# One token tile's gates by scatter DMAs in place of one-hot matmuls, in a hybrid attention and PEER encoder layer

## The chip, the cores and the metric

The kernel runs on one core of a Trainium2 chip. The metric is the device time of one execution in microseconds (us), here the median of three runs of the kernel before. One more execution was recorded by the hardware profiler, and every row shown below is from it. TensorE (PE) does matmuls, VectorE (DVE), ScalarE (ACT) and GpSimd (POOL) elementwise work; SyncE (SP), ACT and POOL issue DMAs.

## The reference

Two sequences, 256 prompt tokens and 512 sample tokens of width 1024, go through one encoder layer: RMS norm, one large projection, banded and dilated attention, gates and an output projection, and then a PEER layer. The change lies in the PEER layer of the sample. There each token picks, for each of 8 heads, 16 experts out of 16384, and adds gate times gelu(u·h) times v of each:

```python
idx = (e1 * PEER_KEYS + e2).reshape(T, PEER_HEADS * PEER_TOPK)
g = jax.nn.softmax(top, axis=-1).reshape(T, PEER_HEADS * PEER_TOPK)
...
u = expert_u[ic]
a = jax.nn.gelu(jnp.einsum('ted,td->te', u, tc, ...), approximate=False)
vv = expert_v[ic]
return jnp.einsum('te,ted->td', (gc * a).astype(tc.dtype), vv)
```

So a token has 128 pairs of expert and gate; two heads can pick the same expert, and then their gates add up. The result is to be that of fp32, which the kernel gets from three fp32r matmuls of high and low parts.

## The kernel before, in words

**Stages.** The prompt's front (norm, projection, attention, output projection, query and top 16) runs from 0 to about 315 us of the span, the sample's front to about 886 us, woven with the prompt's PEER layer. That layer gathers: `gather` (L790 to L816) fetches with one indirect DMA per slot the u row, later the v row, of 128 tokens (128 rows, 512 KB, issued by POOL at L799), and DVE multiplies it in at L806 or L814. 512 such gathers last nearly to the end of the kernel; they are the filler that is woven into all that follows.

**The sample's PEER layer** is dense. Each expert is computed for all 512 tokens. (1) The u blocks (`stage1`, L730): 128 blocks of 128 experts; each loads 512 KB of u (`ur`, by SP), is split into `uh` (ACT) and `ul` (DVE, L140), takes 24 matmuls of 128x512 into `pu`, a gelu (L740), and is stored to `ad` in DRAM. `uh` and `ul` have four buffers each. Eight blocks run first; the rest, from the generator `ua`, are woven into (2) and (3).

(2) The picks (`pick`, L634): for each of four tiles of 128 sample tokens, DVE finds the 128 experts and gates. POOL computes a table of candidate indices `ce` (L653, L655) that DVE needs further on in the same pick. At its end the pick turns indices and gates into five tables `sl` with a transpose (L695 to L701).

(3) The gate matrix (`gbuild`, L704): one row of 16384 experts per token, nonzero at the token's picks. It is built as one fp32 matmul per token, of two one-hot 128x128 matrices (`o1` with the expert's upper index, `o2` with its lower index times the gate, built at L712 to L722 on DVE and ACT), which leaves two PE records per token, 1024 in all. ACT copies the result (`p_g`) into `gs` and stores it by 2 MB DMAs into `gd`, four for each token tile.

(4) The dense stage (`dense`, L743): for each of 128 blocks of experts SP loads v (`vr`), the gelu values (`gl` from `ad`), and for each eight blocks the gates (`gt` from `gd`, 2 MB); DVE multiplies `gl` with `gt` at L761, the product and v are split into two parts each, and 24 matmuls go into the accumulators `held`.

**What sets the order.** `ORDER` (L40) lists the picks ("p") and gate tiles ("b"). `fill` (L818) advances a stage and takes one u block for so much of its work (`UP`, `UB`); `weave` takes `GB` gathers per unit of gate work, and `GV` gathers per unit of the dense stage. A scheduler then orders each engine's instructions; each engine runs its own list in order, so an instruction that waits holds back all that follow it on that engine. A gather also waits for an `anchor` (the last gelu or split issued when it was written) that paces it.

Of the kernel before, what the change touches and what calls it, by code (L numbers as in the profile page):

```python
# [21 lines left out]
D = 1024  # L22
# [17 lines left out]
IPW = 0.4  # L40
MU = 0.9
PGP, PGS = (0.5, 0.45)
ORDER, SLB = ('pppbpbbb', 3)
U0, UP, UB = (8, 0.45, 1.0)
GB, GV = (2.4, 2.0)


@with_exitstack
def tile_peer(ctx: ExitStack, tc: tile.TileContext, a: dict):
# [21 lines left out]
    ident = cp.tile([128, 128], F32, name="ident")  # L71
    make_identity(nc, ident)
    iota = cp.tile([128, 128], F32, name="iota")
    posx = cp.tile([128, NCAND], BF16, name="posx")
    ropeC = cp.tile([128, 6, 16], F32, name="ropeC")
    ropeS = cp.tile([128, 6, 16], F32, name="ropeS")
# [4 lines left out]
    def consts():  # L81

        nc.sync.dma_start(ropeC, a["ropeC"])
        nc.sync.dma_start(ropeS, a["ropeS"])
        g16 = cp.tile([128, 4, 16], F32, name="g16")
        nc.sync.dma_start(g16, a["gains"][:, 0:16].unsqueeze(0).broadcast_to([128, 4, 16]))
        gc = cp.tile([128, 4], F32, name="gc")
        for h in range(2):
            nc.sync.dma_start(gc[64 * h:64 * h + 64, :], a["gains"].rearrange("k d -> d k"))
            ve.memset(gc[64 * h:64 * h + 16, :], 1.0)  # L90
        for i, k in enumerate(("k_norm_a", "q_norm_a", "q_norm_b", "k_norm_b")):
            c = cp.tile([128, 6, 16], F32, name="rc" + k)
            s = cp.tile([128, 6, 16], F32, name="rs" + k)
            g = g16[:, i:i + 1, :]
            ve.tensor_tensor(c, ropeC, g.broadcast_to([128, 6, 16]), op=ALU.mult)
            ve.tensor_tensor(s[:, :, 0:8], ropeS[:, :, 0:8], g[:, :, 8:16].broadcast_to([128, 6, 8]), op=ALU.mult)
            ve.tensor_tensor(s[:, :, 8:16], ropeS[:, :, 8:16], g[:, :, 0:8].broadcast_to([128, 6, 8]), op=ALU.mult)
            rope[k] = (c, s)
            gcol[k] = gc[:, i:i + 1]
        nc.sync.dma_start(sink, a["sink"].unsqueeze(0).broadcast_to([128, 8]))  # L100
        ve.tensor_scalar_mul(nsink, sink, -1.0)
        nc.sync.dma_start(iota, a["iota"])
        nc.sync.dma_start(posx, a["posx"])
        yield 0

    def gain(pool, k):
# [11 lines left out]

    xs = dr.tile([S_S, D], F32, name="xs")
    sgd = dr.tile([2, 2, 4, 128, 512], F32, name="sgd")  # L120
    gd = dr.tile([S_S // GCH, 128, 128, GCH], F32, name="gd")

    anchor, turn, tog = [None], [0], [0]

# [205 lines left out]
    def front(seq):  # L330
# [6 lines left out]
        with ExitStack() as fs:  # L337
# [23 lines left out]
            with tc.tile_pool(name="att" + seq, bufs=1, reuse_waits="tile") as ap_:  # L361
# [170 lines left out]
                                         es.unsqueeze(2).broadcast_to([128, 4, 64]), op=ALU.mult)  # L532

                if seq == "p":
                    more = chain(norm1("s", tTh, tTl, "right"), gates_pre(PIECES, Th, Tl, nt, put),
                                 gates_pre(PIECES[:GS[0]], tTh, tTl, 4, put_s))
                else:
                    more = gates_pre(PIECES[GS[1]:], Th, Tl, nt, put_s)
# [95 lines left out]
    def pick(pool, seq, t, vv, iu):  # L634
# [47 lines left out]
        wt = pool.tile([128, 8, 16], F32, tag="wt", name="wt", bufs=1)  # L682
        ve.tensor_tensor(wt, tv, tv[:, :, 0:1].broadcast_to([128, 8, 16]), op=ALU.subtract)
        gates(pool, wt)
        ei = pool.tile([128, 128], I32, tag="ei", name="ei", bufs=1)
        ve.tensor_copy(ei, ex.rearrange("p h s -> p (h s)"))
        ii = pool.tile([128, 128], I32, tag="ii", name="ii", bufs=1)
# [12 lines left out]
        for j in range(1, 3):  # L700
            ac.mul(sl[t][2 + j], p[:, j * 128:(j + 1) * 128], -1.0)  # L701
        yield 2

    def gbuild(pool, t):  # L704
        for c in range(128 // GCH):
            gs = pool.tile([128, 128, GCH], F32, tag="gs", name="gs", bufs=2)
            for q in range(0, GCH, 4):
                p = (ps_tr, ps_o)[q // 4 % 2]("p_g")
                t4 = c * GCH + q
                if q % 8 == 0:  # L710
                    o1 = pool.tile([128, 8, 128], F32, tag="o1", name="o1", bufs=B1)
                    ve.tensor_tensor(o1, iota.unsqueeze(1).broadcast_to([128, 8, 128]),  # L712
                                     sl[t][0][:, t4:t4 + 8].unsqueeze(2).broadcast_to([128, 8, 128]), op=ALU.is_equal)
                for j in range(4):
                    tk = t4 + j
                    tg = {"a": "o2a", "v": "o2"}[BY[tk % len(BY)]]
                    o2 = pool.tile([128, 128], F32, tag=tg, name=tg, bufs=B2 if tg == "o2" else B3)
                    if tg == "o2a":
                        ac.activation(o2, iota, AF.Abs, bias=sl[t][3][:, tk:tk + 1])
                        ac.activation(o2, o2, AF.Relu, bias=sl[t][2][:, tk:tk + 1], scale=sl[t][4][:, tk:tk + 1])  # L720
                    else:
                        ve.tensor_scalar(o2, iota, sl[t][1][:, tk:tk + 1], sl[t][2][:, tk:tk + 1], op0=ALU.is_equal, op1=ALU.mult)  # L722
                    pe.matmul(p[:, j * 128:(j + 1) * 128], lhsT=o1[:, q % 8 + j, :], rhs=o2, start=True, stop=True)
                ac.copy(gs[:, :, q:q + 4].rearrange("p e t -> p t e"), p.rearrange("p (t e) -> p t e", e=128))
                yield 0.6
            nc.scalar.dma_start(gd[t * (128 // GCH) + c], gs)

    ad = dr.tile([128, 128, S_S], F32, name="ad")

# [13 lines left out]
    def dense(pv_, psd):  # L743
# [4 lines left out]
        def stage2(j):  # L748
            g, b = divmod(j, GRP)
            if b == 0:  # L750
                gts[g] = pv_.tile([128, S_S // GCH, GRP, GCH], F32, tag="gt", name="gt", bufs=2)
                nc.sync.dma_start(gts[g], gd[:, :, g * GRP:(g + 1) * GRP, :].rearrange("c p e t -> p c e t"))
            vr = pv_.tile([128, D], F32, tag="vr", name="vr", bufs=5)
            nc.sync.dma_start(vr, vrows[j])
            ga = pv_.tile([128, S_S], F32, tag="gl", name="gl", bufs=4)
            nc.sync.dma_start(ga, ad[j])
            vh = pv_.tile([128, D], F32R, tag="vh", name="vh", bufs=3)
            vl = pv_.tile([128, D], F32R, tag="vl", name="vl", bufs=3)
            split(vh, vl, vr)
            gv = ga.rearrange("p (c t) -> p c t", t=GCH)  # L760
            ve.tensor_tensor(gv, gv, gts[g][:, :, b, :], op=ALU.mult)  # L761
            ph = pv_.tile([128, S_S], F32R, tag="ph", name="ph", bufs=3)
            pl = pv_.tile([128, S_S], F32R, tag="pl", name="pl", bufs=3)
            anchor[0] = split(ph, pl, ga)
            return ph, pl, vh, vl
# [101 lines left out]
    with tc.tile_pool(name="gb", bufs=1, reuse_waits="tile") as gpool:  # L867
        slp.append(gpool)
        gp2.append((gpool, 2))
        P = [pick(pks["s"][1], "s", t, *tops["s"][t]) for t in range(4)]  # L870
        B = [gbuild(gpool, t) for t in range(4)]
        due = [0.0]
        it = {"p": iter(P), "b": iter(B)}
        for k in ORDER:
            g = next(it[k])
            fill(weave(g, gg, GB) if k == "b" else g, ua, UP if k == "p" else UB, due)
        run(ua)
        gp2.append((None, 0))
    pks["s"][0].__exit__(None, None, None)
# [29 lines left out]
def _layout(inputs):  # L909
# [26 lines left out]
    o["ropeS"] = np.concatenate([-s, s], axis=1).astype(np.float32).reshape(6, 128, 16).transpose(1, 0, 2)  # L936
    import ml_dtypes
    o["posx"] = np.broadcast_to(np.arange(NCAND).astype(ml_dtypes.bfloat16), (128, NCAND))
    o["iota"] = np.broadcast_to(np.arange(128, dtype=np.float32), (128, 128))
    o["maskA_s"], o["maskB_s"], o["maskO_s"] = _masks(_SEQ_S, _PERM_S[:128], 4)  # L940
    o["maskA_p"], o["maskB_p"], o["maskO_p"] = _masks(_PERM_P, _PERM_P[:128], 2)
# [22 lines left out]
```

## Time and profile before

| | us |
|---|---|
| median of 3 runs | 2473.23 (2470.12 to 2475.72) |
| the profiled execution | 2468.71 |
| its span, first to last instruction | 2466.9 |
| PE busy in the span | 2350.8 (95%) |
| DVE busy | 1886.5 (76%) |
| ACT busy | 1076.1 (44%) |
| POOL busy | 812.1 (33%) |

Read it as follows: the profiled execution lies 4.5 us under the median of the runs, and 1.8 us of it lie outside the span. Shares of busy time are means over stages with different limits, so the rows below are taken stage by stage: from about 960 to 1054 us the picks and u blocks run, from 1054 to about 1600 the gates, u blocks and gathers, to 1725 the last u blocks and the turn to the dense stage, and from there the dense stage with gathers. Where PE's busy time equals the length of its window, PE has no idle time in it, and where the window is longer, the rest is PE waiting.

### The profile page before, as it was taken

To read this page: it belongs to the slowest core of one execution; us is meant where nothing else is said; L and a number is where in the kernel's file an instruction comes from. 1 tells how busy PE (TensorE), PEld (TensorE's weight loads), DVE (VectorE), ACT (ScalarE), POOL (GpSimd) and SP (SyncE) were. 2 spreads that over 40 slices of the span, in tenths; PEclk is the share of its full clock that TensorE was granted. 3 is DMA by queue.
4 is the path that set the end of the run, shared out by engine and by line. 5 is a ranking of instruction groups with operands and counts; after the bars stand their busy time and mean duration, and the time that the engine had idled before them with its cause. 6 is when DMAs were issued, how large, how long until landed. Compare 5 with 4: busy or idle time off the path is not lost. (4 is left out here: it accounts for less than half of the span.)

```text
span 2466.9 us, 34172 instructions
## 1 busy us (share of the span) xinstructions
PE 2350.8 (95%) x11926; PEld 1964.5 (80%) x11926; DVE 1886.5 (76%) x4013; ACT 1076.1 (44%) x1848; POOL 812.1 (33%) x624
## 2 busy tenths in 40 slices
PE   8998998999998999999999999997999999999999
PEld 6787877877887888888888888876888777777777
DVE  6765699677688889978579889853787888789873
ACT  5764435434433344367466666732222222222222
POOL 0000320345555401044144544420444443444310
PEclk9999999989998999999999999999999999999999
DMA  6423542467787434479789999995899999999972
GB/s 214 145 87 128 179 136 73 151 224 224 271 280 262 137 107 137 152 289 370 250 305 372 358 352 341 339 375 211 322 392 368 343 349 352 356 353 371 376 268 103
DMA packets 246365, 642.79 MB, mean 261 GB/s; under 512 B 22576, under 2 KB 77488, under 8 KB 244144
## 3 DMA queue, kind: packets, MB, share of 16 engines
q1 hardware_dynamic: 151728, 305.02, 36.4%
q0 software_dynamic: 73728, 268.47, 30.0%
q10 hardware_dynamic: 20736, 67.12, 6.8%
q8 instruction: 94, 1.54, 0.3%
q14 instruction: 79, 0.65, 0.1%
HBM read 561.60 MB, written 77.59 MB: 259 GB/s over the span
## 5 line engine op out<-in xcount | busy, mean ns | idle before, releaser
L799 POOL DMA_INDIRECT gr<-u,pidx x256 | 329.0, 1285 | 558.9 <-ACT ph L139 168.1
L799 POOL DMA_INDIRECT gr<-v,pidx x256 | 333.4, 1302 | 459.9 <-ACT ph L139 196.2
L144 PE MATMUL held<-vh,ph 128*128 128x512 f32 x1024 | 403.0, 394 | 31.3 <-ACT ph L139 30.7
L144 PE MATMUL pu<-tTh,uh 128*128 128x512 f32 x1024 | 407.4, 398 | 14.2 <-ACT uh L139 14.2
L146 PE MATMUL pu<-tTh,ul 128*128 128x512 f32 x1024 | 401.3, 392 | 4.1 <-DVE ul L140 4.1
L806 DVE SCALAR_TENSOR_TENSOR gr<-gr,tok 128x1024 f32<-128x1024 f32 x256 | 330.8, 1301 | 96.7 <-DMA gr<-u,pidx 96.5
L145 PE MATMUL held<-vl,ph 128*128 128x512 f32 x1024 | 400.8, 391 | 0.0
L145 PE MATMUL pu<-tTl,uh 128*128 128x512 f32 x1024 | 400.6, 391 | 0.0
L814 DVE SCALAR_TENSOR_TENSOR x<-gr,act,x 128x1024 f32<-128x1024 f32 x256 | 327.4, 1279 | 42.5 <-DMA gr<-v,pidx 40.6
L146 PE MATMUL held<-vh,pl 128*128 128x512 f32 x1024 | 314.9, 389 | 0.0
L144 PEld LDWEIGHTS held<-vh,ph 128*128 128x128 f32 x1024 | 193.9, 189 | 78.3 <-ACT ph L139 37.2
L140 POOL TENSOR_TENSOR wlo<-wraw,whi 128x1024 fp32r<-128x1024 f32 x51 | 128.6, 2522 | 376.8 <-ACT whi L139 373.8
L139 ACT CAST vh<-vr 128x1024 fp32r<-128x1024 f32 x128 | 134.5, 1051 | 257.0 <-PE held L146 154.2
L144 PEld LDWEIGHTS pu<-tTh,uh 128*128 128x128 f32 x1024 | 193.8, 189 | 53.2 <-ACT uh L139 15.9
L140 DVE TENSOR_TENSOR vl<-vr,vh 128x1024 fp32r<-128x1024 f32 x128 | 156.5, 1222 | 102.4 <-ACT vh L139 98.4
L146 PEld LDWEIGHTS pu<-tTh,ul 128*128 128x128 f32 x1024 | 193.3, 189 | 46.2 <-DVE ul L140 6.1
L145 PEld LDWEIGHTS held<-vl,ph 128*128 128x128 f32 x1024 | 193.8, 189 | 40.0
L146 PEld LDWEIGHTS held<-vh,pl 128*128 128x128 f32 x1024 | 192.2, 188 | 40.0
L145 PEld LDWEIGHTS pu<-tTl,uh 128*128 128x128 f32 x1024 | 193.5, 189 | 37.6
L139 ACT CAST whi<-wraw 128x1024 fp32r<-128x1024 f32 x137 | 143.8, 1050 | 167.7 <-DMA wraw<-w_in 52.7
L139 ACT CAST uh<-ur 128x1024 fp32r<-128x1024 f32 x128 | 133.8, 1050 | 175.7 <-PE pu L145 92.7
L139 ACT CAST ph<-gl 128x512 fp32r<-128x512 f32 x128 | 79.4, 620 | 267.0 <-DVE gl L761 106.5
(400 smaller groups left out, 4565.5 us busy)
## 6 DMA issues: line engine op xcount, KB each, us to landing
ur<-ublk SPq DMA_DIRECT2D x128, 512.0 KB
vr<-v SPq DMA_DIRECT2D x128, 512.0 KB
wraw<-w_in SPq DMA_DIRECT2D x80, 512.0 KB
gd<-gs ACTq DMA_DIRECT2D x16, 2048.0 KB
gt<-gd SPq DMA_DIRECT2D x16, 2048.0 KB
gl<-ad SPq DMA_DIRECT2D x128, 256.0 KB
wraw<-w_query SPq DMA_DIRECT2D x32, 512.0 KB
wraw<-w_out SPq DMA_DIRECT2D x16, 512.0 KB
```

The lines of the kernel that those rows point to most:

```text
L139: i = ac.copy(hi, src)
L140: eng.tensor_tensor(lo, src, hi.bitcast(F32), op=ALU.subtract)
L144: pe.matmul(out, lhsT=lh, rhs=rh, start=first, stop=False)
L145: pe.matmul(out, lhsT=lh, rhs=rl, start=False, stop=False)
L146: pe.matmul(out, lhsT=ll, rhs=rh, start=False, stop=last)
L799: st = gp.indirect_dma_start(out=g, out_offset=None, in_=tab, in_offset=bass.IndirectOffsetOnAxis(ap=pidx[t][:, s:s + 1], axis=0))
L806: ve.scalar_tensor_tensor(g, g, 1.0, tok, op0=ALU.mult, op1=ALU.mult, accum_out=act[:, s:s + 1])
L814: ve.scalar_tensor_tensor(xt, g, act[:, s:s + 1], xt, op0=ALU.mult, op1=ALU.add)
```

## The change

Token tile 0 no longer goes through the gate matmuls. Its pick makes an index `si` = expert * 128 + token (the constant `pcol` is the token's number) and a copy of the gates `w0`, and no tables `sl`. A generator `scatter` then issues on POOL 128 indirect DMAs, one per slot, each of which adds 128 gates of 4 bytes into 128 cells of `gx` in DRAM. All 128 write `gx`, so the program makes each wait until the one before it has landed. Before that `gx` is zeroed: `clear` sets a 128x1024 tile to zero and stores it 16 times (512 KB each, issued by POOL), as filler of the prompt's attention, ahead of the sample's norm. `gbuild` runs for tiles 1 to 3 only, and `gd` shrinks to 12 stores. The dense stage loads `gt` in two DMAs (512 KB from `gx`, 1.5 MB from `gd`) and multiplies in two steps of 128 and 384 columns. `ORDER` has one "b" less, and `UB`, `GB` and the new `SC` set how many u blocks, gathers and scatters go to a unit of gate work.

```diff
@@ -40,9 +40,9 @@
 IPW = 0.4
 MU = 0.9
 PGP, PGS = (0.5, 0.45)
-ORDER, SLB = ('pppbpbbb', 3)
-U0, UP, UB = (8, 0.45, 1.0)
-GB, GV = (2.4, 2.0)
+ORDER, SLB = ('pppbpbb', 3)
+U0, UP, UB = (8, 0.45, 1.33)
+GB, GV, SC = (3.1, 2.0, 2.25)
 
 
 @with_exitstack
...
@@ -118,7 +120,9 @@
 
     xs = dr.tile([S_S, D], F32, name="xs")
     sgd = dr.tile([2, 2, 4, 128, 512], F32, name="sgd")
-    gd = dr.tile([S_S // GCH, 128, 128, GCH], F32, name="gd")
+
+    gx = dr.tile([128 * 128 * 128, 1], F32, name="gx")
+    gd = dr.tile([(S_S - 128) // GCH, 128, 128, GCH], F32, name="gd")
 
     anchor, turn, tog = [None], [0], [0]
 
@@ -532,7 +536,7 @@
                                          es.unsqueeze(2).broadcast_to([128, 4, 64]), op=ALU.mult)
 
                 if seq == "p":
-                    more = chain(norm1("s", tTh, tTl, "right"), gates_pre(PIECES, Th, Tl, nt, put),
+                    more = chain(clear(), norm1("s", tTh, tTl, "right"), gates_pre(PIECES, Th, Tl, nt, put),
                                  gates_pre(PIECES[:GS[0]], tTh, tTl, 4, put_s))
                 else:
                     more = gates_pre(PIECES[GS[1]:], Th, Tl, nt, put_s)
@@ -682,6 +686,14 @@
         wt = pool.tile([128, 8, 16], F32, tag="wt", name="wt", bufs=1)
         ve.tensor_tensor(wt, tv, tv[:, :, 0:1].broadcast_to([128, 8, 16]), op=ALU.subtract)
         gates(pool, wt)
+        if t == 0:
+            si = pool.tile([128, 128], I32, tag="si", name="si", bufs=1)
+            ve.tensor_scalar(si, ex.rearrange("p h s -> p (h s)"), 128.0, pcol, op0=ALU.mult, op1=ALU.add)
+            w0 = pool.tile([128, 128], F32, tag="w0", name="w0", bufs=1)
+            ac.copy(w0, wt.rearrange("p h s -> p (h s)"))
+            slots.extend((si, w0))
+            yield 2
+            return
         ei = pool.tile([128, 128], I32, tag="ei", name="ei", bufs=1)
         ve.tensor_copy(ei, ex.rearrange("p h s -> p (h s)"))
         ii = pool.tile([128, 128], I32, tag="ii", name="ii", bufs=1)
@@ -700,6 +712,26 @@
         for j in range(1, 3):
             ac.mul(sl[t][2 + j], p[:, j * 128:(j + 1) * 128], -1.0)
         yield 2
+
+    slots = []
+
+    def scatter():
+
+        si, wt = slots
+        for k in range(128):
+            gp.indirect_dma_start(out=gx, out_offset=bass.IndirectOffsetOnAxis(ap=si[:, k:k + 1], axis=0),
+                                  in_=wt[:, k:k + 1], in_offset=None, compute_op=ALU.add)
+            yield 1
+
+    def clear():
+
+        z = gpl.tile([128, D], F32, tag="gr", name="zero", bufs=3)
+        gp.memset(z, 0.0)
+        v = gx.rearrange("(p q d) o -> q p (d o)", p=128, d=D)
+        for q in range(16):
+            st = gp.dma_start(v[q], z)
+            tc.add_manual_dep(st.ins, anchor[0].ins.name, SYNC, reason="pace")
+            yield 0.1
 
     def gbuild(pool, t):
         for c in range(128 // GCH):
@@ -723,7 +755,7 @@
                     pe.matmul(p[:, j * 128:(j + 1) * 128], lhsT=o1[:, q % 8 + j, :], rhs=o2, start=True, stop=True)
                 ac.copy(gs[:, :, q:q + 4].rearrange("p e t -> p t e"), p.rearrange("p (t e) -> p t e", e=128))
                 yield 0.6
-            nc.scalar.dma_start(gd[t * (128 // GCH) + c], gs)
+            nc.scalar.dma_start(gd[(t - 1) * (128 // GCH) + c], gs)
 
     ad = dr.tile([128, 128, S_S], F32, name="ad")
 
@@ -748,8 +780,12 @@
         def stage2(j):
             g, b = divmod(j, GRP)
             if b == 0:
-                gts[g] = pv_.tile([128, S_S // GCH, GRP, GCH], F32, tag="gt", name="gt", bufs=2)
-                nc.sync.dma_start(gts[g], gd[:, :, g * GRP:(g + 1) * GRP, :].rearrange("c p e t -> p c e t"))
+                gt = pv_.tile([128, S_S * GRP], F32, tag="gt", name="gt", bufs=2)
+                g0 = gt[:, 0:128 * GRP].rearrange("p (e t) -> p e t", t=128)
+                g1 = gt[:, 128 * GRP:].rearrange("p (c e t) -> p c e t", e=GRP, t=GCH)
+                nc.sync.dma_start(g0, gx.rearrange("(p e t) o -> p e (t o)", e=128, t=128)[:, g * GRP:(g + 1) * GRP, :])
+                nc.sync.dma_start(g1, gd[:, :, g * GRP:(g + 1) * GRP, :].rearrange("c p e t -> p c e t"))
+                gts[g] = g0, g1
             vr = pv_.tile([128, D], F32, tag="vr", name="vr", bufs=5)
             nc.sync.dma_start(vr, vrows[j])
             ga = pv_.tile([128, S_S], F32, tag="gl", name="gl", bufs=4)
@@ -757,8 +793,9 @@
             vh = pv_.tile([128, D], F32R, tag="vh", name="vh", bufs=3)
             vl = pv_.tile([128, D], F32R, tag="vl", name="vl", bufs=3)
             split(vh, vl, vr)
-            gv = ga.rearrange("p (c t) -> p c t", t=GCH)
-            ve.tensor_tensor(gv, gv, gts[g][:, :, b, :], op=ALU.mult)
+            gv = ga[:, 128:].rearrange("p (c t) -> p c t", t=GCH)
+            ve.tensor_tensor(ga[:, 0:128], ga[:, 0:128], gts[g][0][:, b, :], op=ALU.mult)
+            ve.tensor_tensor(gv, gv, gts[g][1][:, :, b, :], op=ALU.mult)
             ph = pv_.tile([128, S_S], F32R, tag="ph", name="ph", bufs=3)
             pl = pv_.tile([128, S_S], F32R, tag="pl", name="pl", bufs=3)
             anchor[0] = split(ph, pl, ga)
@@ -868,12 +905,14 @@
         slp.append(gpool)
         gp2.append((gpool, 2))
         P = [pick(pks["s"][1], "s", t, *tops["s"][t]) for t in range(4)]
-        B = [gbuild(gpool, t) for t in range(4)]
+        B = [gbuild(gpool, t) for t in range(1, 4)]
+        sc = (x for f in (scatter,) for x in f())
         due = [0.0]
         it = {"p": iter(P), "b": iter(B)}
         for k in ORDER:
             g = next(it[k])
-            fill(weave(g, gg, GB) if k == "b" else g, ua, UP if k == "p" else UB, due)
+            fill(weave(weave(g, gg, GB), sc, SC) if k == "b" else g, ua, UP if k == "p" else UB, due)
+        run(sc)
         run(ua)
         gp2.append((None, 0))
     pks["s"][0].__exit__(None, None, None)
```

POOL's list at the end of the picks: `ce` is the candidate table of a pick, `gr` a gather's tile; `pidx_85` and `pidx_86` are the prompt tiles' indices. Before:

```order
L653 TENSOR_TENSOR ce<-fi,i_11830 128x8x3
L653 TENSOR_TENSOR ce<-fi,i_11830 128x8x2 x3
L655 TENSOR_TENSOR ce<-i_11830,fi 128x8x8
L799 DMA gr<-u,pidx_85 128x1024 x22
L799 DMA gr<-v,pidx_85 128x1024 x128
L799 DMA gr<-u,pidx_86 128x1024 x128
```

After the change; `gx<-w_9658,si` is a scatter of `w0` by the index `si`:

```order
L657 TENSOR_TENSOR ce<-fi,i_12120 128x8x3
L657 TENSOR_TENSOR ce<-fi,i_12120 128x8x2 x3
L659 TENSOR_TENSOR ce<-i_12120,fi 128x8x8
L722 DMA gx<-w_9658,si 2097152x1 x20
L836 DMA gr<-u,pidx_86 128x1024
L722 DMA gx<-w_9658,si 2097152x1 x2
L836 DMA gr<-u,pidx_86 128x1024 x2
L722 DMA gx<-w_9658,si 2097152x1
L836 DMA gr<-u,pidx_86 128x1024 x2
L722 DMA gx<-w_9658,si 2097152x1
```

Where the gathers followed the last `ce` directly, 20 scatters now stand between, and two groups of 12 stand ahead of the two last `ce` tables, so 44 scatters are ahead of the first gather of this stage. Behind it one or two scatters stand between every one to four gathers.

SP's list at the turn from u blocks to the dense stage, from its second load of `gt` on (`ur` u blocks, `vr` v blocks, `gl` gelu values). Before, 14 `ur` loads stand directly ahead of the first `gt`, and these follow later:

```order
L754 DMA vr<-v 128x1024
L752 DMA gt<-gd 128x16x256
L732 DMA ur<-ublk 128x1024 x2
L754 DMA vr<-v 128x1024
L756 DMA gl<-ad 128x512
```

After the change, from the store of the first prompt tile's output on:

```order
L853 DMA y<-x_81 128x1024
L764 DMA ur<-ublk 128x1024 x19
L786 DMA gt<-gx 128x1024
L787 DMA gt<-gd 128x12x256
L790 DMA vr<-v 128x1024
L792 DMA gl<-ad 128x512
```

The last eight `ur` loads (two here, six some rows further on) stood behind loads for the dense stage; now all 128 stand ahead of the first `gt`, which waits for the last scatter.

## Rows read from the trace of the kernel before

**Rows 1.** The page: the span, its busy engines, and GB/s in the 40 slices.

```profile
span 2466.9 us, 34172 instructions
...
PE 2350.8 (95%) x11926; PEld 1964.5 (80%) x11926; DVE 1886.5 (76%) x4013; ACT 1076.1 (44%) x1848; POOL 812.1 (33%) x624
...
GB/s 214 145 87 128 179 136 73 151 224 224 271 280 262 137 107 137 152 289 370 250 305 372 358 352 341 339 375 211 322 392 368 343 349 352 356 353 371 376 268 103
```

**Rows 2.** Windows: stretch, length, busy PE, PEld, DVE, ACT, POOL, then clock, DMA share, GB/s.

```profile
120.00:315.00 195.00, 179.19 (x1234) 160.01 (x1232) 120.70 (x380) 100.53 (x186) 25.33 (x11) 0.98 0.40 131
960.00:1054.00 94.00, 94.00 (x425) 77.94 (x424) 92.73 (x228) 39.43 (x69) 6.78 (x18) 1.00 0.45 149
1054.00:1600.00 546.00, 546.00 (x2904) 469.95 (x2903) 441.46 (x652) 363.77 (x662) 238.82 (x170) 1.00 0.90 331
1600.00:1725.00 125.00, 108.12 (x469) 87.50 (x467) 58.25 (x79) 37.76 (x49) 21.53 (x18) 0.93 0.81 300
1725.00:1950.00 225.00, 224.31 (x990) 185.68 (x990) 175.03 (x257) 64.81 (x81) 101.17 (x77) 1.00 0.96 355
1950.00:2370.00 420.00, 393.03 (x1711) 320.68 (x1710) 345.24 (x380) 117.31 (x145) 175.95 (x142) 1.00 0.97 357
```

**Rows 3.** Windows of the u blocks without gates, and with gates.

```profile
900.00:1050.00 150.00, 150.00 (x666) 124.16 (x665) 149.22 (x459) 61.57 (x96) 11.76 (x36) 1.00 0.47 151
1250.00:1600.00 350.00, 350.00 (x1892) 302.29 (x1891) 302.96 (x440) 243.81 (x447) 162.16 (x119) 1.00 0.94 348
```

**Rows 4.** Windows, the same stretch, instructions on tile `p_g` alone (one-hot matmuls).

```profile
1250.00:1600.00 350.00, 85.46 (x692) 84.95 (x691) 97.12 (x87) 1.00 0.94 348
```

**Rows 5.** Lines by form: mean ns of one for two DVE operations.

```profile
L722 DVE TENSOR_SCALAR o<-iota,sl,sl 128x128 f32<-128x128 f32 x320 | 97.0, 350 | 17.7 <-PE p_g L723 15.2 <-PE pu L146 1.5
...
L761 DVE TENSOR_TENSOR gl<-gl,gt 128x512 f32<-128x512 f32 x128 | 87.4, 685 | 23.3 <-DMA gl<-ad 23.0
```

**Rows 6.** Timeline of POOL: start, length, idle before and its releaser.

```profile
982.59 3.07 POOL L653 TENSOR_TENSOR ce<-fi,i 128x128 f32<-128x128 f32 x8 [29.96 <-DVE pr L674]
...
1054.06 1.64 POOL L799 DMA_INDIRECT gr<-u,pidx  x1 [33.69 <-ACT ga__10423 L740]
1062.18 2.66 POOL L799 DMA_INDIRECT gr<-u,pidx  x1 [6.48 <-ACT ga__10507 L740]
...
1068.35 0.94 POOL L799 DMA_INDIRECT gr<-u,pidx  x1 [0.30 <-issue]
```

**Rows 7.** Timeline of DVE at the turn from picks to gates.

```profile
954.40 0.21 DVE L686 CAST ei<-ex 128x128 int32<-128x128 f32 x1
...
1053.66 1.22 DVE L140 TENSOR_TENSOR ul<-ur,uh 128x1024 fp32r<-128x1024 f32 x1
...
1059.75 1.23 DVE L806 SCALAR_TENSOR_TENSOR gr<-gr,tok 128x1024 f32<-128x1024 f32 x1 [2.33 <-DMA gr<-u,pidx]
...
1069.15 1.23 DVE L806 SCALAR_TENSOR_TENSOR gr<-gr,tok 128x1024 f32<-128x1024 f32 x1 [5.13 <-DMA gr<-u,pidx]
```

**Rows 8.** Timelines of POOL and DVE, two gathers while the DMAs are little loaded.

```profile
444.50 1.05 POOL L799 DMA_INDIRECT gr<-u,pidx  x1 [5.48 <-ACT whi L139]
450.99 0.94 POOL L799 DMA_INDIRECT gr<-u,pidx  x1 [5.44 <-DVE ssq L382]
...
448.98 1.23 DVE L806 SCALAR_TENSOR_TENSOR gr<-gr,tok 128x1024 f32<-128x1024 f32 x1 [3.10 <-DMA gr<-u,pidx]
...
455.81 1.23 DVE L806 SCALAR_TENSOR_TENSOR gr<-gr,tok 128x1024 f32<-128x1024 f32 x1 [1.45 <-DMA gr<-u,pidx]
```

**Rows 9.** Waits of DVE, 1054 to 1600 us: total, times, longest.

```profile
DVE x L814 <- DMA gr<-v,pidx: 40.6, 23, 6.0
...
DVE gr L806 <- DMA gr<-u,pidx: 19.6, 6, 5.1
```

**Rows 10.** Waits of PE, 1590 to 1760 us, in the same columns.

```profile
PE pu L144 <- ACT uh L139: 13.5, 3, 9.7
```

## What the change is predicted to do

> **What bounds the kernel now.** I began with the page: PE is busy for 2350.8 of 2466.9 us, so the kernel is mostly bound by matmuls, and a cut in PE work can pay [rows 1]. But shares are means, so I read the windows by stage. From 1054 to 1600 us, where the gates are built, PE is busy in all 546.00 us, and from 960 to 1054 in all 94.00: whatever leaves PE there shortens the kernel, and whatever makes it wait there lengthens it [rows 2]. The DMAs are loaded to 0.90 with gates and to 0.45 before them; POOL works 238.82 of 546 us. At 1600 to 1725, the turn to the dense stage, PE is idle for 16.9 us at a clock of 0.93. In the dense stage PE is busy in 393.03 of 420 us. Next I asked the timeline where POOL and DVE pass from picks to gates, since the change puts its new work there [rows 6, 7]. DVE is full in that stretch (149.22 of 150 us, PE 150.00) [rows 3]. At 1053.66 it makes one more `ul`, and at 1059.75 it uses the first gather, issued at 1054.06.
>
> **What the change removes: the one-hot matmuls.** Without gates, PE passes 666 matmuls in 150 us, 0.2252 us each. With gates it passes 1892 in 350 us, of which 692 are on `p_g` [rows 3, 4]. The other 1200 take 270.2 us, so one of `p_g` takes (350 - 270.2)/692 = 0.115 us. Tile 0 has 128 tokens of two records, 256: 29.5 us less, in a stretch where PE never waits. The 32 one-hot DVE and ACT sets that go with them lie beside PE, and so do the four 2 MB stores.
>
> **What it adds: a serial chain on POOL.** Each of 128 scatters waits until the one before has landed, and POOL works its list in order, so behind a waiting scatter stand the `ce` tables of tiles 2 and 3, which DVE needs for its picks, and all gathers, which DVE uses ahead of further `ul`, and PE waits for `ul`. 44 scatters stand ahead of the first gather of this stage. The period P of one is not in the trace. The nearest row is a gather at light load: issued at 444.50 and used at 448.98, and 450.99 and 455.81, so 4.48 and 4.82 us, 4.65 in the mean, from issue to the moment DVE stops waiting for it [rows 8]. A gather moves 524288 bytes; at the page's best slice, 392 GB/s [rows 1], that is 1.34 us, which a scatter of 512 bytes does not have. POOL takes 0.30 us from one issue to the next [rows 6]. So P = 4.65 - 1.34 + 0.30 = 3.6 us. The bounds: below, issue alone, 0.94 + 0.30 = 1.24 us, if landing cost nothing [rows 6]; above, a gather in the loaded stretch, 1062.18 to 1069.15, 6.97 us [rows 6, 7], which stands also for 128 small read and add steps costing as much as 128 rows. I take 3.6 because this stretch is loaded to 0.45 only, near the light case.
>
> The Trainium skill, "DMA: Bandwidth & Descriptors", section "Anatomy of one DMA — SWDGE (gpsimd) path", gives a fixed cost of about 2.0 us per DMA, most of it the receipt from the memory written, plus bytes over 436 GB/s. By it a gather would take 3.2 us, where the rows have 4.65. As an estimate from that page, with 0.94 us of issue ahead, P would be 2.94 and the sum near 2460 instead of 2489. No row here is of a scatter, and on the gather the row disagrees with the rule by 1.4 us, so I go by the rows.
>
> Now the stall. The index is ready at the place of the `ei` of before, 954.40 [rows 7], so the chain starts at 955. 44 periods and about 7 us for the two `ce` groups behind it (3.07 us and a little each [rows 6]) put the first gather at 955 + 44 × 3.6 + 7 = 1120; 5.7 us later (1054.06 to 1059.75) DVE has it: 1126 instead of 1059.75, 66 us late. `uh` and `ul` have four buffers, so PE can work through four blocks, 4 × 24 × 0.2252 = 21.6 us, before it waits. The stall is 66 - 21.6 = **45 us**; each 1 us of P moves it by 44, and below P = 2.58 there is none. At P = 6.97 it is 193. The u blocks have no other source of work for PE here, since gates and `ul` stand behind the same DVE instruction.
>
> **The other parts.** The turn at 1600: SP's list now has all `ur` loads ahead of the first `gt`, where eight stood behind loads for the dense stage. Of the idle 16.9 us PE waited 13.5 for `uh`, behind those loads [rows 2, 10]. I take half of 16.9 back, -8.5; bounds 0 and -16.9. The last scatter, which the first `gt` awaits, is at the list's end ahead of 229 gathers and should be done by then.
>
> The other 84 scatters lie among the gathers: 84 × (0.94 + 0.30) = 104 us more on POOL, which has 307 free in 546 [rows 2]. DVE waits 40.6 + 19.6 = 60 us for gathers there now, and PE for none of it [rows 9]; half as many DMAs again (84 beside 170) may add 30. I charge a quarter, +7, since the lead is used up by the stall; bounds 0 and 30.
>
> Dense stage: 9 gathers more than before are left for it (229 for 220). PE's idle 27 us over 142 gathers is 0.19 each: +2. The product in two steps costs DVE 0.350 for 128 columns [rows 5] and, by the slope (685 - 350)/384 = 0.87 ns, 0.573 for 384: 0.24 more, 128 times, 31 us on an engine with 75 of 420 free [rows 2, 5]. PE hides it: 0; if not, the 6% in which PE waits make it 2.
>
> Clearing writes 8.4 MB in the prompt's front, where the DMAs are loaded to 0.40 [rows 2]: 0. If each of 16 stores held up its stretch for issue and transfer, 16 × (0.94 + 1.34) = +36. DVE's `si` replaces five operations of a pick: 0.
>
> **Sum.** -29.5 + 45 - 8.5 + 7 + 2 = +16. On the profiled execution, 2468.7, that is 2484.7; on the median of the runs, which lies 4.5 higher and which I forecast, 2473.2 + 16 = **2489**.
>
> **The rivals.**
> - *B, the chain is cheap.* If P is 2.6 or less, the first gather is there before PE has used up its lead, and the whole gain of the matmuls stays: -29.5 - 8.5 + 7 + 2 = -29, **2444**. For it: 512 bytes are next to nothing beside 512 KB. Against it: no indirect DMA in the rows is that quick. The price at P = 3.6 is 45 us, the point from which it decides 2.58. With P up to 3.1 the kernel is still faster by over 0.2%. The rule of the Trainium skill cited above, in "Anatomy of one DMA — SWDGE (gpsimd) path", would end in this case.
> - *C, a scatter costs what a loaded gather does.* 128 cells in 128 places, each read, added to and written back, may take as long as rows of 4 KB: P = 6.97, 193 in place of 45, **2637**. For it: no row of a scatter excludes it. Against: its row is of a stretch loaded to 0.90, and the chain runs where the load is 0.45 [rows 2].
> - *D, the parts cancel*: at P = 3.2 the stall is 28.5, the sum 0, **2473**.
> - *E, the clearing is not hidden*: +36 on the forecast, **2525**. For it: it stands ahead of the sample's norm in the filler, and POOL issues it before other work. Against: a DMA load of 0.40.
>
> **How the numbers follow.** The forecast has 0.43 (its own range 2473 to 2520, P from 3.3 to 4.3), B with P up to 3.1 has 0.33, D 0.10, C 0.09, E 0.05. A measurement of this kernel tells 0.2% from no change, 4.9 us. Faster is B and a little of D: 0.37. Same is most of D and the lower edge of the forecast: 0.10. Slower is the rest: 0.53. The range for 8 in 10 runs from somewhat under B, 2437, where the turn is given back whole, to 2550, P = 5, which leaves C out.
>
> **What would show it.** The timeline of POOL has the scatters at an even distance from 955 us on: that distance is P. If the forecast holds, the first gather of the stage starts near 1120, DVE waits some 50 us ahead of its first gather multiply, and PE has one idle stretch of about 45 us near 1080 to 1125, with all of the time before 954 unchanged. The one-hot term is right if the matmuls on `p_g` are 256 fewer, still at 0.115 us, with PE full from there to the end of the u blocks. The turn is right if PE's wait for `uh` there falls from 13.5 to about 5. The forecast is wrong if PE has no such gap (B), if the distance is 5 or more (C), or if the sample's front starts later than before (E).

## The result and the profile after

The changed kernel takes 2567.14 us in the median of 6 runs (2560.42 to 2581.97), the kernel before 2471.68 (2465.58 to 2475.72, 6 runs): 95 us between the medians. The ratio is 1.0398 with a 95% interval of 1.0368 to 1.0427. Forecast were 2489 and a range up to 2550. The profiled execution took 2577.29 us, which is at the upper end of the runs, and its span is 108.6 us longer than before; the sums below are made within it.

The page of the changed kernel: span, busy engines, and the scatters' line (busy us, mean ns, idle before).

```profile
span 2575.5 us, 33676 instructions
...
PE 2343.2 (91%) x11667; PEld 1949.9 (76%) x11667; DVE 1854.1 (72%) x4041; ACT 1013.3 (39%) x1713; POOL 1078.1 (42%) x769
...
L722 POOL DMA_INDIRECT gx<-w,si x128 | 243.7, 1904 | 238.5 <-DMA gx<-w,si 205.0
```

PE is busy for 7.6 us less than in [rows 1], and for a smaller share of a longer span. A scatter keeps POOL for 1.904 us, and POOL then sits idle for 205 us in all until scatters land.

Windows of the changed kernel by stage, columns as in [rows 2]; the dense stage's first matmul starts at 1825.0, before at 1725.8.

```profile
954.00:1160.00 206.00, 135.67 (x591) 111.68 (x590) 111.13 (x259) 56.73 (x95) 101.46 (x73) 0.82 0.41 96
1160.00:1650.00 490.00, 464.09 (x2283) 393.32 (x2282) 346.80 (x461) 260.56 (x456) 319.18 (x203) 0.96 0.89 306
1650.00:1825.00 175.00, 147.95 (x696) 123.06 (x694) 88.39 (x134) 66.98 (x98) 80.19 (x52) 0.93 0.85 289
1825.00:2575.50 750.50, 711.22 (x3072) 580.72 (x3072) 587.26 (x836) 203.43 (x251) 300.50 (x225) 0.99 0.90 331
```

The same stages of the kernel before; from 954 to 1160 its PE is full.

```profile
1160.00:1650.00 490.00, 485.87 (x2541) 416.23 (x2540) 389.56 (x556) 307.00 (x549) 203.02 (x150) 0.99 0.91 336
1650.00:1725.80 75.80, 62.41 (x262) 49.75 (x260) 25.50 (x29) 21.11 (x28) 4.09 (x4) 0.93 0.69 250
1725.80:2466.90 741.10, 705.40 (x3072) 578.52 (x3072) 565.92 (x690) 202.89 (x251) 277.12 (x218) 0.99 0.90 329
```

The 108.6 us are: 70.3 of PE idle from 954 to 1160 (206.00 - 135.67); 25.9 idle from 1160 to 1650, where 4.1 were; 27.1 idle at the turn, where 13.4 were; 6.6 less PE work up to the dense stage (747.7 for 754.3 busy, by the sums of the rows); and a dense stage 9.4 longer: 70.3 + 21.8 + 13.7 - 6.6 + 9.4 = 108.6. The prompt's front, with the clearing in it, adds little in this trace: the first scatter goes out at 956.87, where `ei` was made at 954.40 before [rows 7].

POOL's timeline in the picks, in the columns of [rows 6]: the first scatters, the two `ce` tables held back, and the last scatters ahead of the first gather.

```profile
956.87 1.61 POOL L722 DMA_INDIRECT gx<-w,si  x1 [3.30 <-ACT wt L632]
960.26 3.20 POOL L722 DMA_INDIRECT gx<-w,si  x1 [1.78 <-DMA gx<-w,si]
...
1006.42 2.39 POOL L657 TENSOR_TENSOR ce<-fi,i 128x128 f32<-128x128 f32 x8
...
1062.45 2.39 POOL L657 TENSOR_TENSOR ce<-fi,i 128x128 f32<-128x128 f32 x8
...
1134.76 1.56 POOL L722 DMA_INDIRECT gx<-w,si  x1 [1.75 <-DMA gx<-w,si]
1138.00 1.56 POOL L722 DMA_INDIRECT gx<-w,si  x1 [1.69 <-DMA gx<-w,si]
1139.86 1.00 POOL L836 DMA_INDIRECT gr<-u,pidx  x1 [0.30 <-issue]
```

DVE in the same stretch.

```profile
1065.13 1.82 DVE L678 TENSOR_TENSOR pr<-eq,ce 128x1600 f32<-128x1600 bf16 x1 [15.50 <-POOL ce L659]
...
1144.09 1.23 DVE L843 SCALAR_TENSOR_TENSOR gr<-gr,tok 128x1024 f32<-128x1024 f32 x1 [52.43 <-DMA gr<-u,pidx]
```

Waits of PE, 954 to 1160 us, in the columns of [rows 10].

```profile
PE p_g L755 <- DVE o L754: 50.6, 2, 41.6
PE pu L150 <- DVE ul L144: 12.2, 1, 12.2
PE pu L148 <- ACT ga__9872 L772: 7.5, 1, 7.5
```

44 scatters take from 956.87 to 1139.86. The first gather goes out there and not at 1054.06 [rows 6], and DVE, whose list holds its multiply ahead of all further `ul` and one-hots `o`, waits 52.43 us for it and uses it at 1144.09, 84.3 us later than before [rows 7]. The two `ce` start at 1006.42 and 1062.45 where they started at 982.59 [rows 6] and, one pick on, 1017.20: DVE waits 35 us for the two in the midst of the picks (15.50 for the second). So PE's 70.3 us are four stops: 7.5 and 12.2 while DVE waits for the `ce` tables, then 41.6 and 9.0 for one-hots that DVE builds behind the first gathers. From 1098 on, when DVE stands and hardly any load runs, the scatters are at an even 3.3 us: 1.56 of POOL and 1.7 of waiting until the one before has landed. Up to 1091, while DVE works and u loads run beside them, the distances go up to 9.3 us.

The scatters behind the first gather do not all lie singly among gathers, as the first rows of POOL's list suggest: 13 of them stand in a row from 1331.25 to 1382.26. The longest waits of DVE for a gather and of PE for DVE, 1160 to 1650 us:

```profile
DVE x L851 <- DMA gr<-v,pidx: 104.3, 40, 24.2
...
PE p_g L755 <- DVE o L754: 25.9, 9, 5.1
```

DVE's longest wait, 24.2 us, is for the first gather behind those 13. PE's idle time in this stage is nine stops of up to 5.1 us, all for DVE.

Matmuls by tile up to the dense stage, before: `pu`, then `p_g`.

```profile
954.00:1725.80 771.80, 658.53 (x2784) 518.88 (x2782) 69.50 (x117) 0.99 0.83 302
...
954.00:1725.80 771.80, 127.13 (x1024) 126.38 (x1024) 142.83 (x128) 0.99 0.83 302
```

The same of the changed kernel.

```profile
954.00:1825.00 871.00, 672.49 (x2788) 530.39 (x2786) 69.38 (x117) 0.92 0.77 253
...
954.00:1825.00 871.00, 106.50 (x768) 103.03 (x768) 106.58 (x96) 0.92 0.77 253
```

The 256 matmuls on `p_g` are gone, but one of the others is now busier: 672.49/2788 = 0.241 us for 0.237 on `pu`, 106.50/768 = 0.139 for 0.124 on `p_g`. For the matmuls that stayed that is 2788 × 0.0047 + 768 × 0.0145 = 24 us more, most of what the one-hots gave back. The granted clock is 0.92 of full speed in the mean, where it was 0.99, so PE spent more time at the lower of the two levels, 1.2 GHz for 2.4: it was at 0.82 in the window with 70 us of idle PE, and at 0.96 in the next. Behind the stop of 12.2 us, for example, the first matmuls on `pu` follow each other at 0.43 us, and later ones at 0.23.

The turn of the changed kernel: POOL, SP's queue, DVE.

```profile
1787.88 1.56 POOL L722 DMA_INDIRECT gx<-w,si  x1 [1.70 <-DMA gx<-w,si]
...
1791.05 0.33 SPq L786 DMA_DIRECT2D gt<-gx  x1
...
1803.40 0.29 DVE L797 TENSOR_TENSOR gl<-gl,gt 128x128 f32<-128x128 f32 x1 [18.72 <-DMA gl<-ad]
```

The last scatter goes out at 1787.88. The first `gt` load, from the matrix that it writes, stands behind all `ur` loads on SP and starts at 1791.05, when it has landed; all loads of the dense stage stand behind it. DVE waits 18.72 us and PE begins at 1825.0.

### The profile page after: what moved, and what is told of

It is laid out like the page before. It is cut to its first block, busy times and chain, and to the rows that moved or that the text cites. A ratio compares the mean times of both kernels' runs of the same rounds, so it can differ in the third digit from the quotient of the medians.

```text
span 2575.5 us, 33676 instructions
## 1 busy us (share of the span) xinstructions
PE 2343.2 (91%) x11667; PEld 1949.9 (76%) x11667; DVE 1854.1 (72%) x4041; ACT 1013.3 (39%) x1713; POOL 1078.1 (42%) x769
## 5 line engine op out<-in xcount | busy, mean ns | idle before, releaser
L836 POOL DMA_INDIRECT gr<-v,pidx x256 | 352.4, 1377 | 281.4 <-ACT ph L143 186.2
L148 PE MATMUL pu<-tTh,uh 128*128 128x512 f32 x1024 | 413.9, 404 | 10.4 <-ACT ga__9872 L772 7.5
L149 PE MATMUL pu<-tTl,uh 128*128 128x512 f32 x1024 | 406.1, 397 | 0.0
L722 POOL DMA_INDIRECT gx<-w,si x128 | 243.7, 1904 | 238.5 <-DMA gx<-w,si 205.0
L150 PEld LDWEIGHTS pu<-tTh,ul 128*128 128x128 f32 x1024 | 196.8, 192 | 60.9 <-DVE ul L144 19.2
```

Source lines behind the costliest of these rows:

```text
L148: pe.matmul(out, lhsT=lh, rhs=rh, start=first, stop=False)
L149: pe.matmul(out, lhsT=lh, rhs=rl, start=False, stop=False)
L150: pe.matmul(out, lhsT=ll, rhs=rh, start=False, stop=last)
L722: gp.indirect_dma_start(out=gx, out_offset=bass.IndirectOffsetOnAxis(ap=si[:, k:k + 1], axis=0), in_=wt[:, k:k + 1], in_offset=None, compu ...
L836: st = gp.indirect_dma_start(out=g, out_offset=None, in_=tab, in_offset=bass.IndirectOffsetOnAxis(ap=pidx[t][:, s:s + 1], axis=0))
```

## The experiments

Three questions: how much of the loss is the scatters' at all, how it divides among their three places in POOL's list (44 ahead of the first gather, 72 among gathers, 12 at the turn), and what a scatter's price is made of. In each expectation, "theory A" is what the account above (the chain, its place in POOL's list, POOL's time) makes of that run, and "rival B" is another cause that would give another time. The kernel before was run again beside each set of runs, so the ratios can be compared between sets.

**Without scatters.** Edit, in `scatter`:

```diff
-            gp.indirect_dma_start(out=gx, ..., compute_op=ALU.add)
+            pass
```

> The changed kernel with its 128 scatters left out (tile 0's gates stay zero, all else as it is: clearing, two loads of gt, two products, the weaving rates). Theory A, the chain of scatters costs all that was lost and the rest is cheap: 29.5 us of one-hot matmuls are gained, nothing stalls ahead of the first gather, and the turn to the dense stage waits for no scatter: 2435 to 2450 us. Rival B, a good part comes from the other edits (clearing, product in two steps, 9 more gathers in the dense stage, rates): above 2475.

Measured: 2447.87 (4 runs) for 2465.85 of before (7 runs), a ratio of 0.9914 (0.9882 to 0.9947). Its windows, one wait of PE (954 to 1704 us), and its matmuls by tile up to the dense stage, `pu`, then `p_g`:

```profile
954.00:1160.00 206.00, 206.00 (x989) 173.31 (x988) 179.59 (x378) 104.92 (x180) 57.11 (x60) 1.00 0.67 236
1160.00:1650.00 490.00, 480.65 (x2414) 407.36 (x2413) 364.17 (x485) 268.52 (x456) 204.72 (x145) 0.99 0.93 338
1650.00:1703.80 53.80, 48.35 (x195) 38.17 (x193) 12.97 (x16) 13.37 (x17) 2.25 (x3) 0.94 0.40 134
...
PE pu L148 <- ACT uh L143: 13.0, 4, 7.1
...
954.00:1703.80 749.80, 667.73 (x2817) 526.56 (x2815) 70.17 (x118) 0.99 0.82 295
...
954.00:1703.80 749.80, 97.96 (x768) 97.40 (x768) 107.81 (x96) 0.99 0.82 295
```

PE is full to 1160, idle for 9.4 us to 1650 and 5.5 at the turn; the dense stage starts at 1703.8. So all of the loss is the scatters', 0.048 of the time of before or about 120 us, and the change without them gains 18 us by the medians, 21 by the ratio (13 to 29). The prediction's rival of a cheap chain had 29, with 7 charged for scatters among gathers.

**Writing in place of adding.**

```diff
-                                  in_=wt[:, k:k + 1], in_offset=None, compute_op=ALU.add)
+                                  in_=wt[:, k:k + 1], in_offset=None)
```

> The changed kernel with scatters that write their value in place of adding it (where two heads pick the same expert, one gate is lost). Theory A, the period is the landing of a DMA that the next one waits for: the distance of scatters that stand alone stays at 3.3 us, 4.1 in the mean ahead of the first gather, and the time within 15 us of the changed kernel's 2567. Rival B, the read and add at the memory make it slow: the distance falls to 2.6 or less and the time to 2500 or less.

Measured: 2485.97, one run. POOL's timeline ahead of the first gather:

```profile
1095.87 0.97 POOL L722 DMA_INDIRECT gx<-w,si  x1 [1.43 <-DMA gx<-w,si]
1098.27 0.97 POOL L722 DMA_INDIRECT gx<-w,si  x1 [1.43 <-DMA gx<-w,si]
1099.54 0.97 POOL L836 DMA_INDIRECT gr<-u,pidx  x1 [0.31 <-issue]
```

Here theory A fell, in the part that the price of a scatter is the landing alone, and rival B's numbers came true (2.6 or less, 2500 or less). A scatter that writes takes POOL 0.97 us and the next waits 1.43 for its landing, 2.40 from one to the next; one that adds takes 1.56 and 1.74, 3.3. So of the 0.9 us that the add costs, 0.6 are POOL's own time and 0.3 the landing. Over the 44 the distance was 3.14 for 4.23 in the mean (43 distances less the two with a `ce` between), the first gather went out at 1099.54 for 1139.86, and PE is idle for 31.8 us to 1160 in place of 70.3. Some 81 us of 95 went, by one run.

**Eight matrices, paced.** Each scatter waits for the eighth before it, and for the last gelu:

```diff
-            gp.indirect_dma_start(out=gx, ...
+            st = gp.indirect_dma_start(out=gz[k % 8], ...
+            tc.add_manual_dep(st.ins, anchor[0].ins.name, SYNC, reason="pace")
```

> The 128 scatters go in turn to 8 separate matrices (not cleared and not read, so tile 0's gates stay zero), so that each waits only for the eighth before it, and each also waits for the last gelu as the gathers do, so that none stands ahead of the first gather; one to three of them stand between every one to three gathers. Theory A, the cost is the wait for landing and the place ahead of the gathers: only issue time is left, 128 x 1.9 = 243 us on POOL beside 240 of gathers in some 520 us; 2440 to 2480, with PE idle under 15 us ahead of 1200. Rival B, issuing 128 small DMAs among gathers is itself what costs: above 2520.

Measured: 2522.99 (4 runs), a ratio of 1.0228 (1.0193 to 1.0263): far outside A's range and, by 3 us, in rival B's, that issuing many small DMAs among gathers is itself what costs. The windows, the scatters' line, and three waits from 1160 to 1650 us, the last from the run without scatters:

```profile
954.00:1160.00 206.00, 200.91 (x958) 168.62 (x957) 163.09 (x342) 96.94 (x168) 91.25 (x69) 0.99 0.66 215
1160.00:1650.00 490.00, 450.57 (x2216) 380.22 (x2215) 337.59 (x445) 254.46 (x442) 383.46 (x237) 0.95 0.89 293
```

```profile
L723 POOL DMA_INDIRECT gz<-w,si x128 | 257.3, 2010 | 39.0 <-issue 31.4 <-DVE o L756 1.5 <-DMA gz<-w,si 0.9
...
DVE x L853 <- DMA gr<-v,pidx: 116.9, 42, 8.6
...
POOL gr L838 <- ACT ga__12509 L774: 32.7, 1, 32.7
...
DVE x L850 <- DMA gr<-v,pidx: 51.9, 27, 5.8
```

The stall ahead of the first gather is gone (5.1 us idle to 1160), and POOL waits 0.9 us in all for a scatter to land. Yet PE is idle for 39.4 us from 1160 to 1650. POOL is busy there for 383.46 us, and each of its 237 instructions is followed by some 0.30 us of issue [rows 6]: 383 + 71 = 454 of 490. Nearly all the rest is one wait of 32.7 us for a gelu. Outside that wait POOL is full, gathers go out late, and DVE waits 116.9 us for those of v, where it waited 51.9 in the same window without scatters. The last two runs take this apart.

**One matrix, paced.** The same pace, `gx` as the target.

> The scatters add into the one matrix as in the changed kernel, but each also waits for the last gelu, which puts none ahead of the first gather and 57, in place of 12, behind the last gather of the gate stage. Theory A, scatters cost where POOL's list holds them alone: no stall ahead of the first gather (PE idle under 10 us from 954 to 1160, in place of 70), but 57 x 3.3 = 188 us at the turn, of which 20 to 40 lie beside the last u blocks: 2590 to 2650. Rival B, the chain is hidden at the turn as the prediction had it: 2500 or less.

Measured: 2612.79, one run. PE's windows:

```profile
954.00:1160.00 206.00, 205.67 (x994) 173.12 (x993) 170.13 (x328) 102.30 (x178) 81.31 (x65) 1.00 0.69 231
...
1650.00:1855.10 205.10, 53.98 (x239) 44.36 (x237) 11.83 (x12) 15.57 (x22) 88.14 (x56) 0.64 0.27 52
```

As A had it: 0.3 us of idle ahead of 1160, and 151 at the turn, where 57 scatters stand alone. With the place in POOL's list the stall moved.

**The first 44 alone, and the first 116.** POOL's list is the changed kernel's, with the rest cut off:

```diff
-        for k in range(128):
+        for k in range(44):
```

> The changed kernel with the first 44 scatters alone (the other 84 are left out, so most of tile 0's gates stay zero); POOL's list is the changed kernel's up to the first gather of the gate stage. Theory A, the stall ahead of that gather is kept to the end: 2448 of the kernel without scatters plus 70 us of PE idle and some 8 at a lower clock: 2510 to 2535. Rival B, PE is idle for as long, but the later stages, which then have fewer late gathers, give it back: under 2490.

> The changed kernel without its last 12 scatters (left out: their gates), which are those that stand alone behind the last gather of the gate stage and ahead of the first load of gt. Theory A, the last scatter holds that load back, and its DMAs stand idle for it: 2567 less 15 to 30, 2535 to 2555. Rival B, the tail lies beside the last u blocks: within 8 us of the changed kernel. What is between this run and that with the first 44 is the cost of scatters among gathers: by A 15 to 40 us.

Measured: 2522.43 (4 runs), 1.0228 (1.019 to 1.0266), and 2554.22 (4 runs), 1.0366 (1.0322 to 1.041). The windows of the first, and its matmuls by tile up to the dense stage, `pu`, then `p_g`:

```profile
954.00:1160.00 206.00, 141.81 (x613) 116.65 (x612) 116.07 (x265) 59.95 (x100) 97.16 (x72) 0.83 0.41 102
1160.00:1650.00 490.00, 488.81 (x2496) 416.70 (x2496) 382.93 (x517) 286.12 (x504) 221.93 (x158) 1.00 0.93 339
...
954.00:1773.90 819.90, 669.73 (x2794) 526.73 (x2792) 69.37 (x117) 0.95 0.77 269
...
954.00:1773.90 819.90, 100.91 (x768) 99.25 (x768) 107.36 (x96) 0.95 0.77 269
```

Of the second:

```profile
954.00:1160.00 206.00, 135.53 (x600) 111.52 (x598) 112.04 (x264) 58.30 (x97) 101.47 (x79) 0.84 0.39 95
1160.00:1650.00 490.00, 469.46 (x2331) 398.08 (x2332) 355.52 (x478) 267.46 (x467) 327.71 (x207) 0.97 0.91 313
1650.00:1813.50 163.50, 145.33 (x656) 118.92 (x654) 85.32 (x132) 60.65 (x87) 55.41 (x38) 0.94 0.82 293
```

With 44 scatters PE loses 64.2 us ahead of 1160 and 1.2 from there to 1650: the stall is not given back. With 116 the second window loses 20.5. In ratios to the kernel before (times 2469 us): without scatters 0.9914, with 44 1.0228, with 116 1.0366, with all 1.0398. The 44 cost 77 us, the 72 from the first gather on 34, the last 12 cost 8. By the widths of the intervals each step is good to some 12 to 14 us, so the last one is not shown by the times: the median lies in A's range for that run, the ratio at the edge of B's. In the traces, one execution each, the dense stage starts at 1813.5 without the 12 and at 1825.0 with them, and PE is idle at the turn for 18.2 us and 27.1.

**What fills POOL.** Eight matrices with the pace again, but with plain writes (that edit without `compute_op=ALU.add`); and five memsets of 128x384 in place of each scatter, with no DMA, of which the first has the pace:

```diff
-            gp.indirect_dma_start(out=gx, ..., compute_op=ALU.add)
+            st = gp.memset(zd, 0.0)
             tc.add_manual_dep(st.ins, anchor[0].ins.name, SYNC, reason="pace")
+            for _ in range(4):
+                gp.memset(zd, 0.0)
```

> The run with 8 separate matrices and a place among the gathers again (tile 0's gates stay zero), but the scatters write and don't add. Theory A, what those scatters cost is POOL's time, which is full there: one takes 1.3 in place of 2.0 us of POOL, 128 x 0.7 = 90 us, and the time falls from 2523 to 2460 to 2490. Rival B, it is the DMA engines, which carry 128 x 128 pieces of 4 bytes either way: 2505 or more.

> The same places in POOL's list, but each scatter is replaced by five small memsets of POOL, of 1.5 to 2.5 us together, and no DMA (tile 0's gates stay zero). Theory A, POOL's time: 2500 to 2540, near the 2523 of the run with scatters to 8 matrices. Rival B, the DMA engines or the landing: 2445 to 2470, near the 2448 without scatters.

Measured: 2477.48 (8 runs), 1.004 (1.0019 to 1.006), and 2508.89 (4 runs), 1.0166 (1.0121 to 1.0211). The line of the plain scatters, and the second window:

```profile
L723 POOL DMA_INDIRECT gz<-w,si x128 | 179.6, 1403 | 42.1 <-issue 34.4 <-DMA gr<-v,pidx 2.9 <-DMA gr<-u,pidx 2.1
```

```profile
1160.00:1650.00 490.00, 470.80 (x2335) 397.67 (x2334) 355.01 (x470) 259.31 (x442) 332.72 (x252) 0.98 0.90 320
```

The line of four of the five memsets (five make 2.13 us), a DVE operation beside them, from 1160 to 1650 us, and the same window:

```profile
L726 POOL MEMSET zd<- 128x384 f32 x512 | 217.5, 425 | 24.1
...
L757 DVE TENSOR_SCALAR o<-iota,sl,sl 128x128 f32<-128x128 f32 x192 | 66.7, 435 | 4.6 <-PE p_g L758 4.6
```

```profile
1160.00:1650.00 490.00, 454.79 (x2250) 384.38 (x2249) 350.74 (x457) 257.45 (x445) 396.93 (x658) 0.97 0.86 301
```

Both as A had it. POOL's work alone, with no DMA, keeps PE idle for 35.2 us of that window, where the scatters to eight matrices left 39.4; with 1.403 in place of 2.010 us of POOL each, it is 19.2. By the times the memsets cost 61 us, the adding scatters 75 and the writing ones 30, all over the 2447.87 without. So what an unchained scatter costs among gathers goes with the time that it takes POOL. The memsets are not a clean stand-in, though: the one-hot step on DVE takes 435 ns beside them, for 350 in [rows 5], some 16 us over the 192 of this window. How much of their 61 us is that, and what the wait for the gelu costs by itself, no run separates.

No run points to a version of this scheme that beats the kernel before: without its scatters the change gains 18 us, and the cheapest placing of 128 of them, plain ones with no chain, costs 30 (2477 for 2448); those leave out the adding that the gates need.

## Why the prediction was wrong

**What stood.** The chain, the first gather behind 44 scatters, and DVE's wait of some 50 us for it (52.43) were as forecast. The product in two steps takes DVE 0.29 and 0.55 us, 0.15 more than before, where 0.24 was charged; what it costs PE is not separated. The clearing was put at 0, and that is good to some 8 us only: the first scatter comes 2 us late here, but in the trace without scatters 33 more matmuls of the u blocks lie behind 954 (2817 for 2784).

**The step that failed first is the period P.** "P = 4.65 - 1.34 + 0.30 = 3.6 us" takes a scatter for a gather without its bytes. With nothing beside it a scatter is at 3.3; the bytes are no error. But up to 1091, with DVE's work and u loads beside it, the distances go up to 9.3 us, and the mean over the 44 is 4.23; which of the two lengthens them is not shown. The prediction had that value in its own range, "P from 3.3 to 4.3". What the row of a gather could not show is that the add costs 0.9 us of each period, as the run with plain writes does. The Trainium skill, "DMA: Bandwidth & Descriptors", section "Anatomy of one DMA — SWDGE (gpsimd) path", has a fixed cost of about 2.0 us per DMA. The plain scatter's 2.40 from one to the next lies 0.4 above that, the adding one's 3.3 by 1.3.

**That the formula then fits is in part luck.** With P = 4.23 it gives 44 × 4.23 - 113.6 = 72 us for 45, and the trace has 70.3. But it makes DVE's first gather 94 us late and lets PE work on for 21.6 of them; measured are 84.3 and 14.0 (84.3 - 70.3). Nor is the stall one stretch near 1080 to 1125: 19.7 us of it are PE's stops at the two `ce` tables, which the prediction names behind the waiting scatters but whose wait it does not price.

**"The other 84 scatters lie among the gathers ... I charge a quarter, +7."** Measured are 21.8 in the profile, and 34 by the runs for 72 of them, near the bound of 30. The working took 0.94 + 0.30 us of POOL for one; it is 1.9 + 0.30, and up to 9.0 us of waiting until the one before has landed. They do not all lie among gathers either: the 13 in a row cost DVE 24.2 us in one wait. POOL's free time, 307 us of 546 [rows 2], was taken for free where it lies between paced gathers.

**"The last scatter ... should be done by then."** It was not: 12 scatters stand together behind the last gather of the gate stage (from 1740.20 on), and SP's order, shown ahead of the prediction, has `gt<-gx` behind all `ur`. That the turn would give 8.5 us back fails with it: +13.7 in the profile. And with no scatter at all PE still waits 13.0 us for `uh`, where it waited 13.5 [rows 10], and is idle for 14.8 us from 1160 to the dense stage, where 17.5 were: SP's order alone gave back some 3 us. Moving the eight late `ur` loads forward left that wait as it was.

**"256: 29.5 us less."** The term was right, and the run without scatters shows it: its `p_g` matmuls take 97.96 us for 127.13, 29.2 less. PE's work ahead of the dense stage falls by only 19.3 there (735.0 for 754.3), mostly because those 33 matmuls of the u blocks, some 8 us, come later. What failed is that stops of PE were priced by their length alone. In the changed kernel PE was busy for only 6.6 us less, because the matmuls that stayed took 24 us longer, with the clock at 0.92. The same sum gives 4 us without scatters and 14 with the first 44 alone. So of the 20 us that the scatters add, about half come with the first stall, the rest with the many short stops behind it.

**Dense stage**: 9.4 us longer for +2, of which 5.8 are busy PE (711.22 for 705.40, for the same 3072 matmuls) and 3.6 idle. It is 5.6 longer without scatters, but 5 shorter than before with the first 116 (2549.6 - 1813.5 = 736.1), where the code of the stage is the same. Single executions differ by that much, so this term is not shown to be off.

Two slips in the working move nothing: by the formula the stall at P = 3.2 is 27 us and not 28.5 (rival D), and the lower bound of the range comes to 2436 and not 2437.

In the profiled execution the miss is 108.6 - 16 = 92.6 us: 25 the period, 15 the scatters among gathers, 22 the turn, 23 the work of PE and its clock, 7 the dense stage. All have one sign; the upper end of the range, P = 5 with all else as forecast, had no room for that.

## What to carry to other kernels

Small DMAs that must wait for each other cost POOL's time and their landing: here, for 512 bytes each, 3.3 us if they add and 2.4 if they write, and more beside other work, with POOL's whole list standing behind each. Count how many stand ahead of the first instruction that a full engine needs, and look for other groups of them further down the list. Before work is moved to a half-idle POOL, add up its busy time with the 0.30 us of each issue in the stage concerned, and test with other POOL work of the same length what that alone costs; look in that test whether DVE's operations keep their length. And price PE's stops, the short ones too, with the clock that follows: the idle time is not all of the loss.

## What was not expected of the hardware

An indirect scatter of 128 pieces of 4 bytes keeps POOL busy for 1.56 us if it adds and 0.97 if it writes, while PE and DVE stand idle and hardly any load runs (1.90 and 1.28 in the mean over the kernel), and the next can start 1.74 and 1.43 us later. Single ones took POOL over 3 us (3.20 at 960.26); why is not shown. Five memsets of POOL, 2.13 us in 128 places, cost the kernel 61 us (2508.89 for 2447.87) with no DMA in them, and DVE's one-hot step beside them took 435 ns for 350.
